# Layer two of a streaming-encoder trunk: pooling and convolution inputs with stationary weights, and eight gate pieces split by transfers

## Chip, cores and metric

One core of a Trainium2 chip runs the kernel. The metric is the device time of one execution in microseconds. The engines are PE (matrix multiplication), DVE (vector), ACT (scalar activation), POOL and SP; POOL and SP work here mainly as the two queues from which transfers are issued.

## What is computed

The reference is a trunk of two equal layers over 256 tokens of width 1024, in float32. What matters here is the first half of a layer:

```python
h = rmsnorm(x, g_pre_mix[l])
(c_q, c_kv, k_r, p_in, s_u, s_v, cv_b, cv_c, cv_x, gate_logits) = split_cols(h @ w_in[l])
y_a = mla_branch(c_q, c_kv, k_r, ...) @ w_br_a[l]
y_b = pool_branch(p_in, pool_w[l], pool_scale[l]) @ w_br_b[l]
y_c = sgu_branch(s_u, s_v, ...) @ w_br_c[l]
y_d = conv_branch(cv_b, cv_c, cv_x, conv_w[l]) @ w_br_d[l]
gates = sigmoid(gate_logits)                    # 4 branches x 1024 channels
merged = gates[:, :, 0] * y_a + gates[:, :, 1] * y_b + gates[:, :, 2] * y_c + gates[:, :, 3] * y_d
x = x + rmsnorm(merged @ w_out[l], g_post_mix[l])
```

The pooling and convolution branches work along time, so they want channels on the partitions and tokens along a row. After this half comes a feed-forward network with a gate (SwiGLU) of the same input width.

## The kernel before

Each float32 number is held as a rounded high part and a low remainder, both of a type that PE multiplies fast; a product is three matmuls, high by high, low by high, high by low (`mac`, L316 to L320). The 256 tokens are two halves `h` of 128.

All weights lie in device memory as 268 pieces of 128 x 1024 numbers in the order of their use (`piece_plan`, L79; `PLAN`). A piece passes three steps. `stage` (L247) issues a transfer from SP's queue into one of four staging tiles `st`. `convert` (L263) has ACT round it into the high tile (L268). `settle` (L283) has DVE subtract the high part from the staged piece into the low tile (L288). High and low tiles share a ring of 24 tiles `u`. `pump` (L290) converts the next piece when two of the 24 are free and keeps the transfers up to four pieces ahead; `W` (L300) hands a piece to the multiplication and frees its tiles after its last use, counted by `uses` (L112).

Work on PE is written out in order. Small generators (attention, pooling, gating, normalisation) are advanced one step at a time between the main groups by `tick` (L338), which also calls `settle` and, with fewer than six unused pieces at hand, `pump`. So the place of every instruction on every engine is fixed by the order in which the program issues it, and each engine takes its own in that order.

The start of layer two: the normalised input lies transposed in four tiles `hh0`, `hl0`, `hh1`, `hl1` (`hT_tiles`, L355), channels on partitions. Groups A (attention inputs) and S (gating unit) come first, then P (`p_in` and `cv_b`, 512 columns) and C (`cv_c` and `cv_x`, 512 columns), both by `group2` (L473) at L964 and L966: the input is the stationary operand, the weights move, and the result has tokens on partitions. ACT scales each result by the token's `rstd` when it leaves PSUM (`evict_p` L930, `evict_c` L934, where DVE also multiplies two convolution inputs). `g_misc` (L779) then turns these results with twelve PE transposes (L789, L793) and three ACT copies per half (L790, L795, L796), so that channels lie on partitions, and goes on with convolution, pooling and gating unit. Meanwhile `g_att` (L769) starts the attention: `g_proj` (L641) takes sums of squares, rotates the key part, finds the reciprocal root (`g_rsqrt`, L400, one start and three steps), scales (L658, L659), and yields `PA` ticks before it transposes.

After C follow the gates of the branches in the order d (convolution), b, c, a: for each branch two column halves of four pieces, `("gd", n, i)` first (L1027). The order of the four pieces over the two halves of tokens is (0,0) (0,1) (1,0) (1,1) (0,2) (0,3) (1,2) (1,3) (`pairs`, L458).

The feed-forward network has, for later blocks of 128 columns, another form of product (`block` L1092, `total` L1106, `g_rrow` L1082): weights stationary, input moving with high and low parts side by side, 512 columns wide, and then 256 columns for the weights' low part. The result has channels on partitions. `total` adds its two halves and multiplies by a row `rrow` that holds `rstd` per token.

Of the kernel before, what the change touches and what calls it, by code (L numbers as in the profile page):

```python
# [41 lines left out]
PA, PB = 2, 4  # L42
# [91 lines left out]
def host_piece(inp, key):  # L134
    l, g = key[0], key[1]
    cols = dict(GROUPS)
    if g in cols:
        return kxn(inp["w_in"][l], 2 * key[2], 2, cols[g])
    if g == "uq":
        return kxn(inp["w_uq"][l], key[2], 1, [c for hd in range(H) for c in q_cols(hd)])  # L140
    if g == "ukv":
        return kxn(inp["w_ukv"][l], 0, 1, [(P * hd, P * hd + 64) for hd in range(H)] +
                   [(P * hd + 64, P * hd + P) for hd in range(H)])
    if g[0] == "g":
        c = 1952 + 1024 * GATE_OF[g[1]] + 512 * key[2]
# [12 lines left out]
    raise KeyError(key)  # L158
# [38 lines left out]
def trunk(ctx: ExitStack, tc, x, xT, wall, small, const, qtab, gpost, out):  # L197
# [92 lines left out]
    def pump(n=1):  # L290

        while n and state["free"] - state["reserve"] >= 2 and state["cv"] < len(PLAN):
            settle(NST - 1)
            stage_to(min(len(PLAN), state["cv"] + NST - len(lows)))
            convert(state["cv"])
            state["cv"] += 1
            state["free"] -= 2
            n -= 1
# [55 lines left out]

    def hT_tiles(h):  # L355
        return T([P, NK, P], f"hh{h}", 1, F32R), T([P, NK, P], f"hl{h}", 1, F32R)
# [253 lines left out]
    class Part:  # L610


        def __init__(self, tiles, s, h):
            self.tiles, self.s, self.h = tiles, s, h

        def __getitem__(self, at):
            k = at[1]
            return self.tiles[k // 2][:, k % 2, self.s, self.h * P:(self.h + 1) * P]

    for l in range(NL):  # L620
# [20 lines left out]
        def g_proj():  # L641
# [24 lines left out]
            yield PA  # L666
# [112 lines left out]
        def g_misc():  # L779
            L = PAD + SEQ  # L780
            zT = tok()[:, :].rearrange("p (c t) -> p c t", c=2)
            cT_ = tok()[:, :].rearrange("p (c t) -> p c t", c=2)
            pT_ = tok()[:, :].rearrange("p (c t) -> p c t", c=2)
            nc.gpsimd.memset(pT_[:, :, 0:PAD], 0.0)
            nc.gpsimd.memset(zT[:, :, 0:PAD], 0.0)
            for h in range(2):
                o = PAD + h * P
                t = tp()
                transposes(t, [z_sb[h][:, 256 + i * P:256 + (i + 1) * P] for i in range(2)])  # L789
                nc.scalar.copy(zT[:, :, o:o + P], t[:, :256].rearrange("p (c t) -> p c t", c=2))  # L790
                yield 1
                t = tp()
                transposes(t, [p_sb[h][:, i * P:(i + 1) * P] for i in range(4)])  # L793
                t4 = t.rearrange("p (c t) -> p c t", c=4)
                nc.scalar.copy(pT_[:, :, o:o + P], t4[:, 0:2, :])  # L795
                nc.scalar.copy(cT_[:, :, o:o + P], t4[:, 2:4, :])  # L796
                yield 1
# [119 lines left out]
        else:  # L917
            o = {}
            for h, i in lead_order(8):
                if h == 1 and i == 0:  # L920
                    finish(turn)
                g, w, ev = (("A", 416, evict_a), ("S", 512, evict_s))[i // 4]
# [20 lines left out]
        pp = [mm(), mm()] if l == 0 else [acc(), acc()]  # L943
        if l == 0:
            def g_evict():
# [7 lines left out]
            for n, (h, i) in enumerate(pairs(4)):  # L953
# [26 lines left out]
        def g_merged(h, q):  # L980
            if q == 0:
# [4 lines left out]
            split_scaled(hh[:, 4 * q:4 * q + 4, :].rearrange("p k t -> p (k t)"),  # L986
                         hl[:, 4 * q:4 * q + 4, :].rearrange("p k t -> p (k t)"), t, 0.5)
# [94 lines left out]
        def g_rrow():  # L1082

            rb = tok()
            for h in range(2):
                nc.vector.tensor_copy(rb[:, h * P:(h + 1) * P], rf[h].to_broadcast([P, P]))
            yield RW
            t = tp()
            transposes(t, [rb[:, h * P:(h + 1) * P] for h in range(2)])
            nc.scalar.copy(rrow, t[:, :SEQ])  # L1090

        def block(key):  # L1092

            pc_ = W((l,) + key)
            o = mm()
            for k in range(NK):
                nc.tensor.matmul(o, pc_[0][:, k * P:(k + 1) * P], hx[k // 2][:, k % 2].rearrange("p s t -> p (s t)"),  # L1097
                                 start=(k == 0), stop=False)
                if k == 5:
                    tick()  # L1100
            for k in range(NK):
                nc.tensor.matmul(o[:, :SEQ], pc_[1][:, k * P:(k + 1) * P], hx[k // 2][:, k % 2, 0, :], start=False,  # L1102
                                 stop=(k == NK - 1))
            return o

        def total(dst, o):  # L1106
            nc.scalar.copy(dst, o[:, SEQ:2 * SEQ])  # L1107
            nc.vector.tensor_tensor(dst, o[:, 0:SEQ], dst, op=ALU.add)  # L1108
            nc.vector.tensor_tensor(dst, dst, rrow, op=ALU.mult)

        def gate_up(b):
            v, sg_ = tok(), tok()
            gv, uv = v[:, 0:SEQ], v[:, SEQ:2 * SEQ]
            o = block(("wg", b))
            if b == B0:
                finish(rr)
            total(gv, o)
# [3 lines left out]
            total(uv, block(("wu", b)))  # L1121
# [19 lines left out]

        gact = [None, None]
        pb, a = {}, {}
        for h, u in lead_order(8):
            if u == 0:
                finish(gturn[h])
                if h == 1:
                    rr = spawn(g_rrow(), 1)
# [81 lines left out]
```

## Time and profile before

| what | value |
|---|---|
| median of 3 runs | 802.87 us (802.28 to 803.49) |
| the profiled execution's own time | 802.21 us |
| its span in the trace | 800.4 us |
| PE busy | 790.8 us (99%) |
| DVE busy | 598.3 us (75%) |
| ACT busy | 452.6 us (57%) |
| POOL busy | 3.9 us (0%) |

The time is that of the whole execution; the span runs from the first to the last instruction of the trace, and the 1.8 us between them lie around it. A busy share is a mean over stages. Matmuls are pipelined, so the recorded duration of one overlaps the next, and the distance between starts tells what one costs. A row of a timeline gives start, duration, engine, line, operation, result and operands, count, and in brackets the idle time before it with what ended it.

### The profile page before, as it was taken

How to read it: one execution, taken by the hardware profiler on the slowest of the kernel's cores; microseconds unless marked ns; L12 is line 12 of the kernel's file. 1: busy time of each engine (PE TensorE's matmuls, PEld its weight loads, DVE VectorE, ACT ScalarE, POOL GpSimd, SP SyncE). 2: the span in 40 equal slices, each digit the busy share in tenths (PEclk: the TensorE clock that was granted, in tenths of full speed). 3: DMA queues.
4: the chain of work that ended last, by engine and by line, in shares of the span. 5: the costliest groups of instructions: out<-in, count | busy, mean ns of one | idle time of the engine just before them, and what ended most of it. 6: DMA issues, size and time to landing. Idle time of an engine off the chain costs nothing.

```text
span 800.4 us, 10903 instructions
## 1 busy us (share of the span) xinstructions
PE 790.8 (99%) x3982; PEld 666.3 (83%) x3982; DVE 598.3 (75%) x1094; ACT 452.6 (57%) x776; POOL 3.9 (0%) x16
## 2 busy tenths in 40 slices
PE   8999999999999999999999999999999999999996
PEld 8888887888888888888888888878888888888885
DVE  6687976758887777778895688764679787777773
ACT  7767655444665555455665675644367555455541
POOL 0000000000000000000000000000000000000000
PEclk9999999999999999999999999999999999999999
DMA  9866444465664565555655545455555555555631
GB/s 317 304 215 212 160 158 158 160 208 164 201 214 136 185 205 185 186 192 176 223 170 197 205 161 182 131 172 197 175 193 184 181 185 186 187 185 185 206 106 52
DMA packets 42245, 148.11 MB, mean 185 GB/s; under 512 B 4688, under 2 KB 5840, under 8 KB 42192
## 3 DMA queue, kind: packets, MB, share of 16 engines
q1 hardware_dynamic: 41328, 145.12, 54.4%
q0 software_dynamic: 576, 2.10, 0.8%
q8 instruction: 31, 0.51, 0.3%
q10 hardware_dynamic: 288, 0.21, 0.1%
q14 instruction: 22, 0.18, 0.1%
HBM read 146.36 MB, written 1.05 MB: 184 GB/s over the span
## 4 chain that ended last, share of the span: by engine, by line
PE 98%; DVE 1%; DMA 0%; ACT 0%; issue 0%; DVEq 0%; SPq 0%; ACTq 0%
PE acc L318 20%; PE acc L320 20%; PE acc L319 20%; PE mm L1097 17%; PE mm L1102 9%; PE tp L440 3%; PE mm L318 2%; PE mm L320 2%; PE mm L319 2%; PE mm L715 1%; PE acc L743 1%; PE acc L909 1%; DMA st<-wall 0%; PE mm L836 0%; PE mm L862 0%; DVE mrg L500 0%
## 5 line engine op out<-in xcount | busy, mean ns | idle before, releaser
L288 DVE TENSOR_TENSOR u<-st,u 128x1024 fp32r<-128x1024 f32 (+1 forms) x268 | 318.6, 1214 | 50.6 <-ACT u L268 50.0
L268 ACT ACTIVATE u<-st 128x1024 fp32r<-128x1024 f32 (+1 forms) x268 | 273.5, 1047 | 17.0 <-DMA st<-wall 16.8
L318 PE MATMUL acc<-u,hh 128*128 128x512 f32 (+1 forms) x424 | 169.1, 399 | 0.0
L320 PE MATMUL acc<-u,hh 128*128 128x512 f32 (+1 forms) x424 | 164.5, 388 | 0.0
L319 PE MATMUL acc<-u,hl 128*128 128x512 f32 (+1 forms) x424 | 164.2, 387 | 0.0
L1097 PE MATMUL mm<-u,u 128*128 128x512 f32 x576 | 144.4, 392 | 0.0
L1097 PEld LDWEIGHTS mm<-u,u 128*128 128x128 f32 x576 | 105.3, 188 | 20.8
L318 PE MATMUL acc<-u,s2k 128*128 128x512 f32 x256 | 101.2, 395 | 0.0
L320 PE MATMUL acc<-u,s2k 128*128 128x512 f32 x256 | 100.6, 393 | 0.0
L319 PE MATMUL acc<-u,s2k 128*128 128x512 f32 x256 | 100.3, 392 | 0.0
L320 PEld LDWEIGHTS acc<-u,hh 128*128 128x128 f32 x424 | 79.6, 188 | 16.2
L318 PEld LDWEIGHTS acc<-u,hh 128*128 128x128 f32 x424 | 79.7, 188 | 14.5 <-issue 0.3
L319 PEld LDWEIGHTS acc<-u,hl 128*128 128x128 f32 x424 | 79.8, 188 | 14.2
L1102 PEld LDWEIGHTS mm<-u,u 128*128 128x128 f32 x576 | 78.6, 190 | 5.6
L1102 PE MATMUL mm<-u,u 128*128 128x256 f32 x576 | 80.3, 282 | 0.0
L1025 ACT ACTIVATE gate<-acc,rhalf 128x512 f32<-128x512 f32 x32 | 22.0, 689 | 65.9 <-PE acc L320 65.7
L320 PEld LDWEIGHTS acc<-u,s2k 128*128 128x128 f32 x256 | 48.1, 188 | 10.1
L318 PEld LDWEIGHTS acc<-u,s2k 128*128 128x128 f32 x256 | 48.2, 188 | 9.3 <-issue 0.3
L319 PEld LDWEIGHTS acc<-u,s2k 128*128 128x128 f32 x256 | 48.1, 188 | 9.1
L1108 DVE TENSOR_TENSOR tok<-mm,tok 128x256 f32<-128x256 f32 x72 | 30.3, 420 | 27.7 <-ACT tok L1107 27.5
L1107 ACT COPY tok<-mm 128x256 f32<-128x256 f32 x72 | 26.6, 370 | 42.6 <-PE mm L1102 39.6
L443 ACT ACTIVATE s2k<-tok 128x256 fp32r<-128x256 f32 (+1 forms) x38 | 16.3, 429 | 53.8 <-DVE tok L1122 53.8
(172 smaller groups left out, 750.1 us busy)
## 6 DMA issues: line engine op xcount, KB each, us to landing
st<-wall SPq DMA_DIRECT2D x261, 512.0 KB, 3.8
st<-wall SPq DMA_DIRECT2D x7, 416.0 KB, 4.0
gpost<-gpost POOLq DMA_DIRECT2D x4, 512.0 KB, 4.7
x<-x SPq DMA_DIRECT2D x2, 512.0 KB, 6.0
small<-small SPq DMA_DIRECT2D x2, 512.0 KB, 4.2
u<-xT SPq DMA_DIRECT2D x3, 256.0 KB, 6.2
st<-wall SPq DMA_DIRECT2D x2, 256.0 KB, 4.3
out<-x SPq DMA_DIRECT2D x2, 256.0 KB, 2.0
```

The source lines that it names most:

```text
L268: nc.scalar.activation(hi[:, :w], st[:, :w], AF.Copy)
L288: nc.vector.tensor_tensor(lo[:, :w], st[:, :w], hi.bitcast(F32)[:, :w], op=ALU.subtract)
L318: nc.tensor.matmul(out_, a[0][aw], w[0][ws], start=start, stop=False)
L319: nc.tensor.matmul(out_, a[1][aw], w[0][ws], start=False, stop=False)
L320: nc.tensor.matmul(out_, a[0][aw], w[1][ws], start=False, stop=stop)
L440: nc.tensor.transpose(dst[:, i * P:(i + 1) * P], s, ident)
L443: nc.scalar.activation(hi, src, AF.Copy)
L1025: nc.scalar.activation(gt[h], pgt[h], AF.Tanh, scale=rhalf[h])
L1097: nc.tensor.matmul(o, pc_[0][:, k * P:(k + 1) * P], hx[k // 2][:, k % 2].rearrange("p s t -> p (s t)"), start=(k == 0), stop=False)
L1102: nc.tensor.matmul(o[:, :SEQ], pc_[1][:, k * P:(k + 1) * P], hx[k // 2][:, k % 2, 0, :], start=False, stop=(k == NK - 1))
L1107: nc.scalar.copy(dst, o[:, SEQ:2 * SEQ])
L1108: nc.vector.tensor_tensor(dst, o[:, 0:SEQ], dst, op=ALU.add)
```

## The change

In layer two only:

1. The P and C groups become eight blocks of 128 columns in the form of the feed-forward network. A piece `(1, "P", i)` or `(1, "C", i)` now holds one block with all of its 1024 rows, and is used once. The input of both halves lies in one tile `hx` of the same total size.
2. `evict_pc` brings each block out with `total`: an ACT copy, a DVE addition, a DVE multiplication by a row `row1` of `rstd` (which `g_rrow` makes beforehand with two transposes), and one further DVE multiplication for the two blocks that are multiplied with another. The results lie at once where `g_misc` put them before, so the twelve transposes and six copies fall away.
3. The eight pieces `("gd", n, i)` of layer two skip the staging tiles: POOL issues a transfer from memory into the high tile (it converts the type on the way), ACT writes the negated high part into the low tile, and POOL issues a second transfer of the same piece that adds to the low tile. DVE has no part in it.
4. `PA` in layer two is three ticks instead of two.

```diff
-PA, PB = 2, 4
+PA, PB = (2, 3), 4
...
-    if key[1] in ("wg", "wu"):
+    if key[1] in ("wg", "wu") or key[0] == 1 and key[1] in ("P", "C"):
         return 1
...
+    if l == 1 and g in ("P", "C"):
+        c = [a + P * i for a, b in cols[g] for i in range((b - a) // P)][key[2]]
+        return kxn(inp["w_in"][l], 0, NK, [(c, c + P)])
...
+        if by_dma(i):
+            state["free"] -= 1
+            staged[i] = U([P, PIECE], F32R)
+            nc.gpsimd.dma_start(staged[i], wall[i, :, :])
+            return
...
+    def by_dma(i):
+
+        key = PLAN[i][0]
+        return key[0] == 1 and key[1] == "gd"
+
     def convert(i):
         key, w = PLAN[i]
+        if by_dma(i):
+            hi, lo = staged.pop(i), U([P, PIECE], F32R)
+            nc.scalar.activation(lo, hi.bitcast(F32), AF.Copy, scale=-1.0)
+            nc.gpsimd.dma_start(lo, wall[i, :, :], accum_op=ALU.add)
+            known(i, hi, lo)
+            return
...
+    def block(key, o, both, high, mid=None):
+
+        pc_ = W(key)
+        for k in range(NK):
+            nc.tensor.matmul(o, pc_[0][:, k * P:(k + 1) * P], both(k), start=(k == 0), stop=False)
...
+        for k in range(NK):
+            nc.tensor.matmul(o[:, :SEQ], pc_[1][:, k * P:(k + 1) * P], high(k), start=False, stop=(k == NK - 1))
+        return o
+
+    def total(dst, o, tmp, rrow):
+
+        nc.scalar.copy(tmp, o[:, SEQ:2 * SEQ])
+        nc.vector.tensor_tensor(tmp, o[:, 0:SEQ], tmp, op=ALU.add)
+        nc.vector.tensor_tensor(dst, tmp, rrow, op=ALU.mult)
...
-            yield PA
+            yield PA[l]
...
-            group2(l, ("P",), hT, pp, 512, evict_p)
-        pc = [acc(), acc()]
-        group2(l, ("C",), hT, pc, 512, evict_c)
...
+                if g == "C" and i >= 2:
+                    total(v[:, 0:SEQ], o, v[:, 0:SEQ], row)
+                    nc.vector.tensor_tensor(dst, dst, v[:, 0:SEQ], op=ALU.mult)
+                else:
+                    total(dst, o, v[:, 0:SEQ], row)
+
+            for i in range(4):
+                o = block((l, "P", i), tp() if i == 2 else mm(), both, high)
+                finish(rr)
+                evict_pc("P", i, o)
+                tick()
+            for i in range(4):
+                evict_pc("C", i, block((l, "C", i), acc(), both, high))
+                tick()
```

On PE, the last block of C and the first two gate pieces of branch d now stand as follows (`L673` is the low part of a block, `L476` a transpose of the attention; `L337`, `L338`, `L339` are the three matmuls of `mac`; the low parts of the first and second gate piece are `u_878` and `u_884`):

```order
L673 MATMUL acc_4353<-hx_3822,u_874_4264 128x256 x8
L476 MATMUL tp_4384<-ident_69,u_805_3949 128x128 x3
L337 MATMUL acc_4405<-u_849_4177,hx_3822 128x512
L338 MATMUL acc_4405<-u_849_4177,hx_3822 128x512
L339 MATMUL acc_4405<-u_878_4296,hx_3822 128x512
L337 MATMUL acc_4405<-u_849_4177,hx_3822 128x512
L338 MATMUL acc_4405<-u_849_4177,hx_3822 128x512
L339 MATMUL acc_4405<-u_878_4296,hx_3822 128x512
L476 MATMUL tp_4413<-ident_69,u_805_3949 128x128 x3
L337 MATMUL acc_4405<-u_854_4204,hx_3822 128x512
L338 MATMUL acc_4405<-u_854_4204,hx_3822 128x512
L339 MATMUL acc_4405<-u_884_4335,hx_3822 128x512
```

Before, the first gate piece stood behind the second half of C with one triple of transposes between two of its units; now both triples stand beside the gate pieces, and the first two low parts are read from the third matmul of their units on.

On ACT, from the copy of the second C block to the negated copy of the fourth gate piece (`L678` is the copy of `total`, `L720`/`L721` scale the attention inputs, `L280` writes a negated high part, `L483` splits a transposed attention input), the order is now:

```order
L678 COPY tok_4309<-acc_4284 128x256
L720 ACTIVATE u_805_3949<-u_805_3949,ry_4256 128x256
L721 ACTIVATE u_805_3949<-u_805_3949,ry_4256 128x128
L720 ACTIVATE u_805_3949<-u_805_3949,ry_4256 128x256
L721 ACTIVATE u_805_3949<-u_805_3949,ry_4256 128x128
L280 ACTIVATE u_884_4335<-u_854_4204 128x1024
L678 COPY tok_4348<-acc_4316 128x256
L280 ACTIVATE u_888_4362<-u_872_4261 128x1024
L678 COPY tok_4375<-acc_4353 128x256
L483 ACTIVATE s2k_4380<-tp_4384,cst_70 128x128 x2
L483 ACTIVATE s2k_4381<-tp_4384,cst_70 128x128
```

Before, the rounding of a gate piece stood behind the same four scalings (`L658`, `L659`), and DVE's subtraction finished the piece. Now the negated copies stand there, and each is followed by a transfer. The negated copy of the fourth gate piece (`u_905`) stands behind six splits (three of them shown).

On DVE the scalings' factor `ry` is made by steps of three small instructions (`L453` to `L455`), and the additions and multiplications of the C blocks (`L679`, `L680`) now stand between these:

```order
L679 TENSOR_TENSOR tok_4276<-acc_4248,tok_4276 128x256
L680 TENSOR_TENSOR tok_4111<-tok_4276,rrow_3906 128x256
L453 TENSOR_TENSOR ra_4257<-ry_4256 128x4
L454 TENSOR_TENSOR ra_4257<-ra_4257,rv_4255 128x4
L455 SCALAR_TENSOR_TENSOR ry_4256<-ra_4257,ry_4256 128x4
L307 TENSOR_TENSOR u_874_4264<-st_4150,u_873_4263 128x1024
L453 TENSOR_TENSOR ra_4257<-ry_4256 128x4
L454 TENSOR_TENSOR ra_4257<-ra_4257,rv_4255 128x4
L455 SCALAR_TENSOR_TENSOR ry_4256<-ra_4257,ry_4256 128x4
L679 TENSOR_TENSOR tok_4309<-acc_4284,tok_4309 128x256
L680 TENSOR_TENSOR tok_4111<-tok_4309,rrow_3906 128x256
L453 TENSOR_TENSOR ra_4257<-ry_4256 128x4
```

Before, two subtractions of weights (`L288`) and no eviction stood between the same steps. The step that begins with the last row shown is the one for which the four scalings wait.

## Rows read from the trace of the kernel before

**Rows 1.** The page's busy times, and its chain that ended last, by engine.

```profile
PE 790.8 (99%) x3982; PEld 666.3 (83%) x3982; DVE 598.3 (75%) x1094; ACT 452.6 (57%) x776; POOL 3.9 (0%) x16
...
PE 98%; DVE 1%; DMA 0%; ACT 0%; issue 0%; DVEq 0%; SPq 0%; ACTq 0%
```

**Rows 2.** Busy us by stretch: length, PE, weight loads, DVE, ACT, POOL, clock, DMA.

```profile
420.00:440.00 20.00, 20.00 (x90) 16.51 (x89) 10.99 (x30) 10.47 (x20) 0.00 (x0) 1.00 0.58 196
440.00:460.00 20.00, 20.00 (x119) 17.49 (x118) 13.52 (x21) 13.09 (x26) 1.02 (x4) 1.00 0.60 208
```

**Rows 3.** Timeline of PE: group S, second half, and the first matmul of group P.

```profile
414.37 0.39 PE L318 MATMUL acc<-u,hh 128*128 128x512 f32 x1
...
421.17 0.39 PE L318 MATMUL acc<-u,hh 128*128 128x512 f32 x1
```

**Rows 4.** The chain in order of time: one block of the feed-forward network, and the next.

```profile
363.34 1.84 PE mm L1097 x8
365.18 0.95 PE mm L1102 x8
366.13 1.84 PE mm L1097 x8
```

**Rows 5.** Timeline of PE: two transposes among matmuls; twelve matmuls of 256 columns.

```profile
448.01 0.38 PE L440 MATMUL tp<-ident,tok 128*128 128x128 f32 x2
448.15 0.48 PE L318 MATMUL acc<-u,hh 128*128 128x512 f32 x1
448.46 0.39 PE L319 MATMUL acc<-u,hl 128*128 128x512 f32 x1
...
449.62 0.28 PE L318 MATMUL mm<-s2k,u 128*128 128x256 f32 x1
...
450.92 0.28 PE L320 MATMUL mm<-s2k,u 128*128 128x256 f32 x1
```

**Rows 6.** Timeline of all engines where a feed-forward block ends.

```profile
648.78 2.00 PE L1097 MATMUL mm<-u,u 128*128 128x512 f32 x8
648.98 0.37 ACT L1107 COPY tok<-mm 128x256 f32<-128x256 f32 x1 [0.53 <-PE mm L1102]
649.38 0.42 DVE L1108 TENSOR_TENSOR tok<-mm,tok 128x256 f32<-128x256 f32 x1
649.84 0.42 DVE L1109 TENSOR_TENSOR tok<-tok,rrow 128x256 f32<-128x256 f32 x1
```

**Rows 7.** Timeline of DVE during group C.

```profile
432.34 0.29 DVE L632 TENSOR_TENSOR tok<-u,cst 128x32 f32<-128x32 f32 x2
...
433.74 0.25 DVE L650 COPY kr<-kr 128x96 f32<-128x96 f32 x1
...
435.26 0.15 DVE L417 TENSOR_TENSOR ra<-ry 128x4 f32<-128x4 f32 x1
...
435.75 1.22 DVE L288 TENSOR_TENSOR u<-st,u 128x1024 fp32r<-128x1024 f32 x1
...
439.27 2.46 DVE L665 COPY u<-tp 64x1024 f32<-64x1024 f32 x2 [0.19 <-PE tp L440]
```

**Rows 8.** Timeline of ACT: scalings, the rounding of a gate piece, splits.

```profile
439.12 0.51 ACT L658 ACTIVATE u<-u,ry 128x256 f32<-128x256 f32 x1 [2.47 <-DVE ry L419]
...
440.52 1.05 ACT L268 ACTIVATE u<-st 128x1024 fp32r<-128x1024 f32 x1
...
447.22 0.37 ACT L447 ACTIVATE s2k<-tp,cst 128x128 fp32r<-128x128 f32 x1 [1.58 <-DVE s2k L448]
448.01 0.37 ACT L447 ACTIVATE s2k<-tp,cst 128x128 fp32r<-128x128 f32 x1 [0.42 <-DVE s2k L448]
```

**Rows 9.** Transfers: SP's queue (packets, MB, share of 16 engines), and issues (count, size, us to landing).

```profile
q1 hardware_dynamic: 41328, 145.12, 54.4%
...
st<-wall SPq DMA_DIRECT2D x261, 512.0 KB, 3.8
...
gpost<-gpost POOLq DMA_DIRECT2D x4, 512.0 KB, 4.7
```

**Rows 10.** The tile gpost: its four transfers from POOL's queue.

```profile
DMA to landing us min/median/max: 3.8/4.7/4.9
```

More of the change, by code (lines that the diff above doesn't have):

```diff
@@ L353, in finish, with __init__, __getitem__ @@
             advance(e)
+    class Part:
+        def __init__(self, tiles, s, h):
+            self.tiles, self.s, self.h = tiles, s, h
+        def __getitem__(self, at):
+            k = at[1]
+            c = np.s_[self.s, self.h * P:(self.h + 1) * P]
+            if len(self.tiles) == 1:
+                return self.tiles[0][:, k, c[0], c[1]]
+            return self.tiles[k // 2][:, k % 2, c[0], c[1]]
+    hx_now = [None]
     def hT_tiles(h):
-        return T([P, NK, P], f"hh{h}", 1, F32R), T([P, NK, P], f"hl{h}", 1, F32R)
+        if h == 0:
+            hx_now[0] = T([P, NK, 2, SEQ], "hx", 1, F32R)
+        return tuple(Part([hx_now[0]], s, h) for s in range(2))
     ident = T([P, P], "ident", 1, pool=cp)
@@ L608, in trunk, with rows_in, rows_out, g_rrow @@
     turn = None
[L610 to L618, printed above, removed]
+    def rows_in(rs):
+        rb = tok()
+        for h in range(2):
+            nc.vector.tensor_copy(rb[:, h * P:(h + 1) * P], rs[h].to_broadcast([P, P]))
+        return rb
+    def rows_out(rrow, rb):
+        t = tp()
+        transposes(t, [rb[:, h * P:(h + 1) * P] for h in range(2)])
+        nc.scalar.copy(rrow, t[:, :SEQ])
+    def g_rrow(rrow, rs):
+        rb = rows_in(rs)
+        yield RW
+        rows_out(rrow, rb)
+    def block(key, o, both, high, mid=None):
+        pc_ = W(key)
+        for k in range(NK):
+            nc.tensor.matmul(o, pc_[0][:, k * P:(k + 1) * P], both(k), start=(k == 0), stop=False)
+            if k == 5:
+                if mid is not None:
+                    mid()
+                tick()
[6 more added lines that the diff above has]
+        nc.vector.tensor_tensor(dst, tmp, rrow, op=ALU.mult)
     for l in range(NL):
@@ L780, in g_misc @@
             L = PAD + SEQ
[L781 to L797, printed above, removed]
+            if l == 0:
+                zT = tok()[:, :].rearrange("p (c t) -> p c t", c=2)
+                cT_ = tok()[:, :].rearrange("p (c t) -> p c t", c=2)
+                pT_ = tok()[:, :].rearrange("p (c t) -> p c t", c=2)
+                nc.gpsimd.memset(pT_[:, :, 0:PAD], 0.0)
+                nc.gpsimd.memset(zT[:, :, 0:PAD], 0.0)
+                for h in range(2):
+                    o = PAD + h * P
+                    t = tp()
+                    transposes(t, [z_sb[h][:, 256 + i * P:256 + (i + 1) * P] for i in range(2)])
+                    nc.scalar.copy(zT[:, :, o:o + P], t[:, :256].rearrange("p (c t) -> p c t", c=2))
+                    yield 1
+                    t = tp()
+                    transposes(t, [p_sb[h][:, i * P:(i + 1) * P] for i in range(4)])
+                    t4 = t.rearrange("p (c t) -> p c t", c=4)
+                    nc.scalar.copy(pT_[:, :, o:o + P], t4[:, 0:2, :])
+                    nc.scalar.copy(cT_[:, :, o:o + P], t4[:, 2:4, :])
+                    yield 1
+            else:
+                zT, cT_, pT_ = zcp
             dh = T([P, 2, SEQ], "s2k", 10, F32R)
@@ L962, in trunk, with both, high, evict_pc @@
                 tick()
-        else:
-            group2(l, ("P",), hT, pp, 512, evict_p)
-        pc = [acc(), acc()]
-        group2(l, ("C",), hT, pc, 512, evict_c)
+            pc = [acc(), acc()]
+            group2(l, ("C",), hT, pc, 512, evict_c)
+        else:
+            zcp = [tok()[:, :].rearrange("p (c t) -> p c t", c=2) for _ in range(3)]
+            for i in (0, 2):
+                nc.gpsimd.memset(zcp[i][:, :, 0:PAD], 0.0)
+            row = row1
+            htile = hx_now[0]
+            def both(k):
+                return htile[:, k].rearrange("p s t -> p (s t)")
+            def high(k):
+                return htile[:, k, 0, :]
+            def evict_pc(g, i, o):
+                dst = zcp[(2 if i < 2 else 1) if g == "P" else 0][:, i % 2, PAD:PAD + SEQ]
+                v = tok()
+                if g == "C" and i >= 2:
+                    total(v[:, 0:SEQ], o, v[:, 0:SEQ], row)
+                    nc.vector.tensor_tensor(dst, dst, v[:, 0:SEQ], op=ALU.mult)
+                else:
+                    total(dst, o, v[:, 0:SEQ], row)
[6 more added lines that the diff above has]
+                evict_pc("C", i, block((l, "C", i), acc(), both, high))
+                tick()
         sm = small_load(l)
@@ L1080, in trunk @@
         rrow = T([P, SEQ], "rrow", 1)
[L1082 to L1109, printed above, removed]
         def gate_up(b):
```

21 lines of the change are left out of this document (13 added, 8 removed).

## Prediction

> **What bounds the kernel now.** I read the page first, then busy time by stretch, then timelines of PE, ACT and DVE around the place of the change. PE is busy for 790.8 of 800.4 us, and the chain that ended last is PE's to 98% [rows 1]. In the two stretches around groups P and C, PE is busy for 20.00 of 20.00 us at full clock, while DVE has 10.99 and 13.52, ACT 10.47 and 13.09, and DMA 0.58 and 0.60 [rows 2]. So no wait is left there to remove. The time changes only with what PE has to do, or with a wait that the change adds. What DVE saves is worth nothing by itself.
>
> **PE's own work.** Groups P and C were 96 matmuls of 512 columns. Thirty such starts lie between 414.37 and 421.17 us, so one costs 0.2267 us [rows 3], and 96 cost 21.76. They become eight blocks of eight matmuls of 512 and eight of 256 columns; such a block takes 366.13 - 363.34 = 2.79 us [rows 4], eight 22.32. That is **+0.56 us**: the columns are the same in number (96 x 512 = 64 x 512 + 64 x 256), so turning the operands saves nothing on PE. Twelve transposes go and two come (for the row of `rstd`). Two transposes put off the matmul behind the next one by 448.46 - 448.01 - 0.227 = 0.22 us [rows 5], 0.11 each; ten fewer are **-1.1 us**. PE's work thus changes by -0.5 us.
>
> **The eviction of blocks and the eight DVE subtractions.** DVE gains eight subtractions of 1.22 us [rows 7] and loses about as much to sixteen additions and multiplications of 0.46 and two products more, less what `evict_c` did. ACT copies 256 columns eight times and loses six turned copies. All of it lies beside PE; if that cover went, it would show as a wait of PE. The transposes' row, the memory of `hx` and the piece layout cost nothing more: the same bytes come on the same queue, and pieces of P and C are read well after they are made.
>
> **The wait that is added.** Before, a gate piece was finished by a subtraction of 1.22 us behind ACT's rounding. Now a transfer L stands in its place, issued by POOL only when ACT has written the negated part. POOL's queue is not what holds it; ACT is, and ACT waits for DVE. I follow the order given above with durations from rows. Group P begins at 421.17 us [rows 3]; two transposes first, so block four ends at 421.17 + 0.22 + 4 x 2.79 = 432.55.
>
> - ACT's copy starts 0.20 us after a block's end, DVE's addition 0.40 behind that, its multiplication 0.46 later [rows 6]: DVE is through with block four at 432.55 + 0.20 + 0.40 + 0.92 = 434.07.
> - DVE then rotates the keys, 433.99 - 432.34 = 1.65; subtracts a weight piece, 1.22; starts the root, 0.49 as a step takes (435.26 to 435.75) [rows 7]; adds and multiplies C's first block, 0.92; one step, 0.49; subtracts, 1.22; one step; C's second block, 0.92; the last step. Sum 7.89: 441.96. (The second block ends at 438.1, so DVE and not PE is late.)
> - ACT scales four times, 1.40, and writes the second gate piece's negated part, 1.05 [rows 8]: the transfer leaves at 444.4.
> - PE wants that piece's low part at 421.17 + 0.22 + 22.32 for the blocks, + 0.22 and 0.66 for eight transposes, + 8 x 0.2267 = 446.4.
>
> So the second piece has 2.0 us for its transfer. For the fourth: ACT copies a block, writes the third piece's negated part (445.8), copies the last block (446.15). DVE, after 2.46 us of key copies [rows 7], does three instructions of 0.46 for each of two blocks, until 447.6. Then splits alternate between ACT and DVE at 0.79 us [rows 8]; with four such turns and two small scalings the fourth negated part is written from 451.0 to 452.1. PE wants it 24 matmuls of 512 columns and twelve of 256 (0.118 each [rows 5]) after the second, at 446.4 + 5.44 + 1.42 = 453.3, plus whatever PE has waited. That leaves 1.2 us. The splits follow transposes that stand ahead of PE's first wait, so that wait doesn't delay them. PE therefore waits **L - 2.0** at the second piece, and after the fourth **L - 1.2 in all**. The first piece has some seven us, the third 4.8 and the wait, those of the second column half over eight: nothing is added there.
>
> **L.** No transfer of the trace adds to its target. The nearest row is `gpost`, 512 KB from the same queue: 3.8 to 4.9, median 4.7 us [rows 9, 10]; a plain piece on SP's queue takes 3.8 [rows 9]. An adding transfer also reads its target. SP's queue moved 145.12 MB in 54.4% of 800.4 us, 333 GB/s, so one more pass over 524288 bytes is 1.6 us: 6.3 if nothing overlaps. I take **5.5**, midway between 4.7 and 6.3. The ends kept are 3.8, a plain landing, and 9.4, two `gpost` landings one after the other.
>
> The Trainium skill ("DMA: Bandwidth & Descriptors", "Anatomy of one DMA — SWDGE (gpsimd) path") fits such a transfer as 2.0 us plus bytes over 436 GB/s. By that L would be an estimated 3.2 us, the wait 2.0 and the time 804.4; the trace's four `gpost` transfers of that size took longer, at least 3.8 us.
>
> **Sum.** -0.5 + (5.5 - 1.2) = +3.8 us. The profiled execution took 802.21, so it would take 806.0; the median of the runs stands 0.66 above it, and 802.87 + 3.8 gives **806.7 us**. With L at 3.8 and 9.4 it is 805.0 and 810.6.
>
> **Rivals.** *No difference* (0.2%, that is 1.6 us, is about what a measurement of this kernel can tell from none). It needs a wait under 2.1 us, L under 3.3, or ACT further ahead than I follow it. For: my chain has some fifteen terms, each good to a few hundredths, and DVE may find its staged pieces earlier. Against: no 512 KB transfer here lands in 3.3 us. Time 802.3 to 804.4; chance 0.20.
>
> *Not slower*: the wait vanishes because DVE reaches the last step of the root early. The place is the three steps between the C blocks; the point is the second negated part written 5.5 us before 446.4, at 440.9 instead of 444.4, and the fourth 4.3 us earlier. Then only PE's -0.5 us is left, 802.3, and at most -1.1 us, 801.8, if the blocks cost what the groups did. Against: the second C block ends only at 438.1, and its eviction, a step, four scalings and the copy (0.6 + 0.92 + 0.49 + 1.40 + 1.05) already end at 442.6. This is part of the case above; that it goes below 801.3 has no row for it, chance 0.06.
>
> *Transfers as the bound*: eight pieces are read twice and eight targets once. Sixteen extra passes of 1.6 us are 25 us of all DMA engines within some 40 us in which 0.4 is free, 16 us. If the nine us of overrun all reach PE besides the 0.5 saved, the time is about 811 to 815. For: POOL's and SP's transfers share the engines. Against: pieces behind these eight are staged over ten us ahead. Chance 0.08.
>
> **How the numbers follow.** The forecast has 0.66, no difference 0.20, a clear gain 0.06, the overload 0.08. Slower by over 0.2% takes the forecast and the overload, 0.74; the same 0.20; faster 0.06. The range runs from 802.2, where the wait is hidden and PE's saving stays, to 811.0, just above L = 9.4. The forecast alone, which holds most of the chance, has 804.4 to 810.6.
>
> **What would show it.** Right: PE idle ahead of the third matmul of the second gate piece, by 2 to 7 us, released by a transfer from POOL, and a smaller gap at the fourth; eight blocks 2.79 us apart; ten transposes fewer; DVE with eight subtractions fewer and still no wait on it. Wrong: PE still without a gap after group C, or its gap ahead of other tiles (staged pieces, PSUM tiles); the adding transfers landing in under 3.3 us; the negated parts written well before 444 us of the old time; blocks slower than 2.79 us.

## The result and the profile after

The changed kernel takes **809.90 us** in the median (808.85 to 811.03), the kernel before 802.87: ratio 1.0086, 95% interval 1.0073 to 1.0100, that is 7.0 us slower. Forecast were 806.7 us and a range of 802.2 to 811.0. Direction and range hold; instead of 3.8 us it lost nearly twice as many. The profiled execution took 808.96 us, 6.75 more than that of before.

The page of the changed kernel, busy times, transfers and issues (to be read beside [rows 1, 9]):

```profile
PE 790.5 (98%) x4004; PEld 664.8 (82%) x4004; DVE 596.1 (74%) x1104; ACT 452.0 (56%) x775; POOL 15.4 (2%) x32
...
q1 hardware_dynamic: 40176, 140.92, 52.1%
q0 software_dynamic: 2880, 10.49, 5.2%
...
PE 89%; DMA 4%; issue 3%; DVE 2%; ACT 1%; POOL 1%; DVEq 0%; ACTq 0%; POOLq 0%
...
u<-wall POOLq DMA_DIRECT2D x16, 512.0 KB, 7.1
```

PE works as long as before, but the chain is PE's to 89% only, where it was 98%, and now runs through transfers, ACT and POOL too. The busy times by stretch, columns as in [rows 2], show where:

```profile
420.00:440.00 20.00, 20.00 (x114) 17.39 (x113) 13.21 (x34) 10.55 (x22) 3.04 (x5) 1.00 0.90 303
440.00:460.00 20.00, 14.18 (x77) 11.33 (x75) 11.52 (x29) 9.55 (x19) 6.86 (x10) 1.00 1.01 259
```

Where PE had 20.00 of 20.00 us it has 14.18; the clock stays at 1.00, and DMA goes from 0.60 to 1.01 (the times of all packets are added up, so the share can pass 1). In the timeline of PE three matmuls waited, each for a transfer, each the third matmul of a unit, which reads a low part. The first two rows are blocks of group P:

```profile
424.30 2.00 PE L667 MATMUL mm<-hx,u 128*128 128x512 f32 x8
...
427.09 2.00 PE L667 MATMUL tp<-hx,u 128*128 128x512 f32 x8
...
446.38 0.40 PE L338 MATMUL acc<-u,hx 128*128 128x512 f32 x1
449.77 0.50 PE L339 MATMUL acc<-u,hx 128*128 128x512 f32 x1 [2.99 <-DMA u<-wall]
...
453.75 0.39 PE L338 MATMUL acc<-u,hx 128*128 128x512 f32 x1
455.53 0.50 PE L339 MATMUL acc<-u,hx 128*128 128x512 f32 x1 [1.39 <-DMA u<-wall]
...
458.17 0.40 PE L338 MATMUL acc<-u,hx 128*128 128x512 f32 x1
460.44 0.50 PE L339 MATMUL acc<-u,hx 128*128 128x512 f32 x1 [1.88 <-DMA u<-wall]
```

From start to start these are 3.39, 1.78 and 2.27 us where 0.227 is usual: 3.16 + 1.55 + 2.05 = **6.8 us** of waits, at the second, third and fourth gate piece. Less 0.5 us of PE work that is 6.3; the last matmul starts 6.3 us later than before (799.07 against 792.74). The rest of the 6.75 lies behind it. One other wait of PE is not in the profile of before: 0.45 us at 39.5 us, for a subtraction in layer one, which the change leaves as it was.

The three transfers by themselves (line L281, one stretch each: the issue, who waited for it, and L, the time from the issue to the landing):

```profile
L281 POOL DMA_DIRECT2D u<-wall x1: 876/876/876, 444.3 to 444.3; - x1
...
  PE acc L339: 3.0, 1
...
DMA to landing us min/median/max: 5.5/5.5/5.5
...
L281 POOL DMA_DIRECT2D u<-wall x1: 1118/1118/1118, 445.5 to 445.5; - x1
...
  PE acc L339: 1.4, 1
...
DMA to landing us min/median/max: 10.0/10.0/10.0
...
L281 POOL DMA_DIRECT2D u<-wall x1: 887/887/887, 451.5 to 451.5; - x1
...
  PE acc L339: 1.9, 1
...
DMA to landing us min/median/max: 8.9/8.9/8.9
```

The second piece's transfer takes the 5.5 us that I took for L. The third's takes 10.0 and the fourth's 8.9. The queues in the stretch from 440 to 460 us (packets, MB, share of 16 engines) show what the engines had to do meanwhile:

```profile
q0 software_dynamic: 1273, 4.65, 93.9%
q1 hardware_dynamic: 144, 0.52, 6.5%
```

POOL's queue (q0) alone nearly fills the engines; SP's (q1) moves one piece.

### The profile page after: what moved, and what is told of

Read it like the earlier page. It is cut to its first block, busy times and chain, and to the rows that moved or that the text cites. A ratio compares the mean times of both kernels' runs of the same rounds, so it can differ in the third digit from the quotient of the medians.

```text
span 807.2 us, 10985 instructions
## 1 busy us (share of the span) xinstructions
PE 790.5 (98%) x4004; PEld 664.8 (82%) x4004; DVE 596.1 (74%) x1104; ACT 452.0 (56%) x775; POOL 15.4 (2%) x32
## 3 DMA queue, kind: packets, MB, share of 16 engines
q1 hardware_dynamic: 40176, 140.92, 52.1%
## 4 chain that ended last, share of the span: by engine, by line
PE 89%; DMA 4%; issue 3%; DVE 2%; ACT 1%; POOL 1%; DVEq 0%; ACTq 0%; POOLq 0%
PE acc L339 18%; PE acc L337 18%; PE acc L338 18%; PE mm L667 17%; PE mm L673 9%; PE tp L476 3%; DMA st<-wall 2%; PE mm L337 2%; PE mm L339 2%; PE mm L338 2%; PE mm L777 1%; DMA u<-wall 1%; DVE u L307 1%; PE acc L805 1%; ACT u L287 1%
## 5 line engine op out<-in xcount | busy, mean ns | idle before, releaser
L307 DVE TENSOR_TENSOR u<-st,u 128x1024 fp32r<-128x1024 f32 (+1 forms) x260 | 309.3, 1214 | 43.6 <-ACT u L287 43.3
L287 ACT ACTIVATE u<-st 128x1024 fp32r<-128x1024 f32 (+1 forms) x260 | 265.3, 1047 | 17.6 <-DMA st<-wall 17.0
L339 PE MATMUL acc<-u,hx 128*128 128x512 f32 (+1 forms) x392 | 152.6, 389 | 6.7 <-DMA u<-wall 6.3
L337 PE MATMUL acc<-u,hx 128*128 128x512 f32 (+1 forms) x392 | 156.4, 399 | 0.0
L338 PE MATMUL acc<-u,hx 128*128 128x512 f32 (+1 forms) x392 | 151.8, 387 | 0.0
L337 PE MATMUL acc<-u,s2k 128*128 128x512 f32 x256 | 100.9, 394 | 0.0
L339 PE MATMUL acc<-u,s2k 128*128 128x512 f32 x256 | 100.6, 393 | 0.0
L338 PE MATMUL acc<-u,s2k 128*128 128x512 f32 x256 | 100.4, 392 | 0.0
L339 PEld LDWEIGHTS acc<-u,hx 128*128 128x128 f32 x392 | 73.6, 188 | 23.9 <-DMA u<-wall 7.6
L337 PEld LDWEIGHTS acc<-u,hx 128*128 128x128 f32 x392 | 73.7, 188 | 13.2 <-issue 0.5
L338 PEld LDWEIGHTS acc<-u,hx 128*128 128x128 f32 x392 | 73.7, 188 | 13.0
L673 PEld LDWEIGHTS mm<-u,u 128*128 128x128 f32 x576 | 78.6, 190 | 5.6
L673 PE MATMUL mm<-u,u 128*128 128x256 f32 x576 | 80.3, 282 | 0.0
L339 PEld LDWEIGHTS acc<-u,s2k 128*128 128x128 f32 x256 | 48.1, 188 | 10.0
L679 DVE TENSOR_TENSOR tok<-mm,tok 128x256 f32<-128x256 f32 x75 | 31.5, 421 | 33.2 <-ACT tok L678 33.0
L337 PEld LDWEIGHTS acc<-u,s2k 128*128 128x128 f32 x256 | 48.2, 188 | 9.3 <-issue 0.2
L338 PEld LDWEIGHTS acc<-u,s2k 128*128 128x128 f32 x256 | 48.1, 188 | 9.2
L678 ACT COPY tok<-mm 128x256 f32<-128x256 f32 x75 | 27.7, 370 | 46.6 <-PE mm L673 43.7
```

What stands on the lines that cost most here:

```text
L307: nc.vector.tensor_tensor(lo[:, :w], st[:, :w], hi.bitcast(F32)[:, :w], op=ALU.subtract)
L337: nc.tensor.matmul(out_, a[0][aw], w[0][ws], start=start, stop=False)
L338: nc.tensor.matmul(out_, a[1][aw], w[0][ws], start=False, stop=False)
L339: nc.tensor.matmul(out_, a[0][aw], w[1][ws], start=False, stop=stop)
L678: nc.scalar.copy(tmp, o[:, SEQ:2 * SEQ])
L679: nc.vector.tensor_tensor(tmp, o[:, 0:SEQ], tmp, op=ALU.add)
```

## The experiments

Two questions were open: which part of the change brings the 7 us, and whether the third and fourth transfer are slow in themselves, late, or in a full queue. The table has the median, the ratio to the kernel before with its interval, and the waits of PE from 440 us on that I read in the profile (start to start, less the usual distance). Small gaps beside a wait, under 0.4 us each, are counted with it in e8, e9, e11 and e12.

| run | kernel | us | ratio (95%) | waits, us |
|---|---|---|---|---|
| | changed | 809.90 | 1.0086 (1.0073 to 1.0100) | 6.8 |
| e1 | layout only | 804.51 | 1.0023 (1.0012 to 1.0035) | 2.3 |
| e2 | transfers only | 808.38 | 1.0068 (1.0053 to 1.0084) | 3.8 + 0.8 |
| e3 | second transfer plain | 807.28 | 1.0054 (1.0040 to 1.0069) | 3.8 + clock |
| e5 | one copy earlier | 808.11 | 1.0068 (1.0054 to 1.0082) | 4.2 + clock |
| e10 | all copies earlier | 807.19 | 1.0059 (1.0044 to 1.0075) | 3.7 + clock |
| e6 | transfers, first half | 805.97 | 1.0040 (1.0026 to 1.0053) | 3.3 |
| e4 | transfers, second half | 803.49 | 1.0011 (1.0002 to 1.0020) | 1.6 |
| e7 | layout, key copies on ACT | 804.10 | 1.0016 (1.0008 to 1.0025) | 2.0 |
| e8 | layout, earlier conversion | 805.30 | 1.0037 (1.0024 to 1.0049) | 2.6 |
| e9 | second half, earlier | 803.60 | 1.0015 (1.0006 to 1.0024) | 1.5 |
| e11 | e9, key copies on ACT | 804.03 | 1.0019 (1.0010 to 1.0028) | 1.7 |
| e12 | e11, one piece earlier | 803.05 | 1.0010 (1.0001 to 1.0019) | 1.4 |

**The parts alone: e1 and e2.** In e1 `by_dma` is false for all pieces; e2 is the kernel before with `by_dma` and its two branches.

```diff
-        return key[0] == 1 and key[1] == "gd"
+        return False
```

> The changed kernel with the eight gate pieces back on the old path (staging tile, ACT rounding, DVE subtraction); pooling and convolution blocks stay as changed. Theory (the loss lies only in three PE waits on adding transfers): those waits, 3.16 + 1.55 + 2.05 = 6.8 us, are gone and PE's own saving of 0.5 us stays: 802.3 us, ratio to the kernel before 0.9993, PE without a gap from 440 to 465 us. Rival (the blocks themselves or their evictions cost, DVE now having blocks and subtractions in one stretch): PE waits on a subtraction or a PSUM tile there, 804 to 810 us.

> The kernel before with only the eight gate pieces by transfers; pooling and convolution groups as before. Theory: the waits come with the transfers alone. The second negated copy ends at about 441.6, its transfer leaves at 441.8 and PE wants it at 444.3, 2.5 us later, so with 5.4 us a wait of 2.9, and further waits at the third and fourth pieces as in the changed kernel, 6 to 7 us in all: 809 to 810 us. Rival (the blocks of the changed kernel make the negated copies late, so that the old groups leave time enough): at most 3 us, 803 to 806.

e1 was slower by 1.7 us, not faster by 0.5: the rival holds. Its timeline of PE:

```profile
448.49 0.50 PE L339 MATMUL acc<-u,hx 128*128 128x512 f32 x1 [0.77 <-DVE u L307]
456.49 0.50 PE L339 MATMUL acc<-u,hx 128*128 128x512 f32 x1 [0.53 <-DVE u L307]
460.99 0.38 PE L337 MATMUL mm<-s2k,u 128*128 128x256 f32 x1 [0.54 <-DVE u L748]
```

DVE is late. The busy times from 434 to 453 us, columns as in [rows 2], before and in e1:

```profile
434.00:453.00 19.00, 19.00 (x99) 15.92 (x98) 14.62 (x31) 12.19 (x26) 1.02 (x4) 1.00 0.58 205
```

```profile
434.00:453.00 19.00, 18.23 (x99) 15.21 (x98) 17.20 (x47) 9.64 (x25) 0.00 (x0) 1.00 0.45 166
```

DVE has 17.20 of 19 us instead of 14.62, in order: the evictions of the blocks stand there beside the subtractions of the gate pieces. In the changed kernel the transfers take these subtractions away, so no wait on DVE shows. e2, the transfers alone, loses 5.6 us, 0.6 below its range: two waits on transfers (2.01 and 1.77 us), and 0.8 us on a product of DVE at 484; where the last us of the loss lies was not found. The times of the two parts add up to about the whole, 1.7 + 5.6 = 7.3 us against 7.0, but the waits behind them are not the same: the changed kernel has none of e1's waits on DVE, and waits 6.8 us on transfers where e2 waits 3.8. In e2 the second piece's transfer left 4.9 us before PE wanted it (441.86 and 446.77), in the changed kernel, where the evictions stand ahead of it on DVE, only 2.4.

**Slow, late or in a queue: e3, e5, e10, e6.** e3 drops the addition; e5 converts one piece earlier; e10 converts all of them earlier; e6 leaves the second half to the old path.

```diff
-            nc.gpsimd.dma_start(lo, wall[i, :, :], accum_op=ALU.add)
+            nc.gpsimd.dma_start(lo, wall[i, :, :])
```

> The changed kernel, but the second transfer writes the piece plainly over the negated copy instead of adding to it; left out is the subtraction of the high part (the low tile holds the whole weight). Same count of transfers, same bytes from memory, same waits and order. In the changed kernel an adding packet of 4 KB takes 328 ns in the middle, a plain or converting one 174. Theory (adding packets take twice as long and fill all DMA engines from 446 us on, which stretches the third and fourth landings to 9 to 10 us): the eight transfers take 8 x 128 x (328 - 174) / 16 = 9.9 us less of all engines; landings of 4 to 5 us, the fourth piece's transfer (leaves at 451.5, wanted at 453.7 without waits) lands at about 456: waits of 2 to 3 us in all, 804.5 to 805.5 us. Rival (a transfer from this queue takes its time whatever it does, what counts is when it leaves): landings of 5.4 to 10 us as now, 808.5 to 810.5.

```diff
-            for _ in g_rsqrt(res, m, 4):
-                yield 1
+            for n, _ in enumerate(g_rsqrt(res, m, 4)):
+                yield pump() or 1 if (l, n) == (1, 3) else 1
```

> The changed kernel with one swap on ACT: the second gate piece's negated copy stands ahead of the four scalings instead of behind them. It then runs at about 438.8 and its transfer leaves at 440.0 instead of 444.25; all else is in the same order. Rival A (only the lateness of a transfer counts, each takes 5.4 us): the second lands at 445.5, before it is wanted at 446.6, the third at 450.9 without a wait, the fourth (leaves at 451.5) at 456.9 against 453.7: one wait of 3.2 us, 805.6 us. Theory (DMA engines are full from 440 us on, the fourth landing is set by the sum of bytes in the queue): the first wait goes, but the later ones take its place, the fourth piece still lands at 458.5 to 460.5: 5 to 6.8 us in all, 807.5 to 809.5 us. Rival B: the second transfer lands no earlier, since the engines serve the first piece's transfer and other pieces up to then: nothing changes, 809.9.

```diff
-                evict_pc("C", i, block((l, "C", i), acc(), both, high))
+                o = block((l, "C", i), acc(), both, high)
+                if i >= 1:
+                    pump()
+                settle()
+                evict_pc("C", i, o)
                 tick()
```

> The changed kernel (all eight gate pieces by transfers) converted earlier in the same way: the second adding transfer leaves at about 440, the third at 444, the fourth at 445.6 instead of 444.25, 445.5 and 451.5. Theory (POOL's queue is served in order and the engines are full from 440 on): the second lands at about 450 to 451 as in the run with one earlier copy, the third at 454 to 455, the fourth at 457 to 458 against a wanted 453.7: waits of 3.5 to 4.5 us, and PE's clock may fall behind a wait of 4 us: 805.5 to 808 us. Rival (lateness is all, a transfer takes 5.4 us from its issue): the fourth lands at 451, no wait is left, 802.3 to 803 us.

```diff
-        return key[0] == 1 and key[1] == "gd"
+        return key[0] == 1 and key[1] == "gd" and key[2] == 0
```

> The changed kernel with transfers only for the four pieces of the first column half; those of the second half go the old way (staging, rounding, subtraction). On POOL's queue the converting transfers of the second half no longer stand between the adding ones. Theory (the queue serves transfers in the order of issue, an adding one alone takes 5.4 to 5.5 us and each transfer ahead of it costs 1.4 to 2.7 us more): the second piece is as late as before (leaves about 444.2, lands 449.7, wait 3.2 us), the third lands at 452 to 453 without a wait of its own, the fourth (leaves 451.5) at 457 to 457.5, a wait of 0.1 to 0.6 more: 3.3 to 3.8 us of waits, and up to 0.9 us for a DVE that again subtracts four pieces: 805.5 to 807 us. Rival (each adding transfer is slow by itself, 9 to 10 us from the third on, whatever stands beside it): 809 to 810 us. Rival B (a wait of 3 us or more also lowers the clock of PE and that is most of the loss): 807 to 809 with matmuls 0.43 us apart behind the wait.

*e3* came out 1.8 us above its range. The waits at the third and fourth piece went, and POOL's queue took 4.0% of the engines' time instead of 5.2%, 9.8 us less of all sixteen, so the addition does cost that. But the second piece still waited for 3.8 us: its plain transfer landed only 6.2 us after its issue, later than the adding one in the same place (5.5), and no run shows why. Behind the wait the matmuls ran 0.43 us apart. By stretch in e3, columns as in [rows 2]:

```profile
445.00:449.00 4.00, 0.52 (x3) 0.09 (x1) 2.24 (x9) 1.75 (x6) 1.08 (x3) 0.90 0.91 308
449.00:455.00 6.00, 5.80 (x14) 4.55 (x15) 2.89 (x6) 3.61 (x5) 2.11 (x4) 0.50 1.01 326
```

From 449.20 to 454.91 us thirteen distances take 5.71 instead of 2.95, so the clock costs 2.8 us there. The wait and the clock together are 6.6 us, of which the median shows less: this one execution was 1.1 us ahead of that of before already at 84 us.

*e5* lies within its forecast (807.5 to 809.5), by another path than written. The transfer left at 440.3 and landed no earlier than in the changed kernel (449.7):

```profile
L281 POOL DMA_DIRECT2D u<-wall x1: 873/873/873, 440.3 to 440.3; - x1
...
DMA to landing us min/median/max: 10.6/10.6/10.6
```

This is rival B for that piece: PE waited there, once, for 4.2 us, and the clock took 1.7 more; no later piece made it wait for more than 0.1 us. Rival A, by which only the time of issue counts, would have given 805.6 and falls. *e10* says the same of all of them: the second and the fourth transfer were issued 5.5 and 5.8 us earlier than in the changed kernel (438.75 and 445.72) and took 11.4 and 13.3 us, so that the fourth landed at 459.0 instead of 460.4, and the time is 807.2 us; lateness alone would have given 802.3 to 803.

*e6* takes the second half's transfers from between the adding ones. It came out at 805.97, in the range of the theory. In its profile the third and the fourth transfer land in 6.5 and 5.4 us:

```profile
L281 POOL DMA_DIRECT2D u<-wall x1: 868/868/868, 445.4 to 445.4; - x1
...
DMA to landing us min/median/max: 6.5/6.5/6.5
...
L281 POOL DMA_DIRECT2D u<-wall x1: 870/870/870, 451.4 to 451.4; - x1
...
DMA to landing us min/median/max: 5.4/5.4/5.4
```

So an adding transfer isn't slow by itself from the third on. In the changed kernel landings follow the order of issue: 449.7 (444.25 + 5.5), 451.7 (a converting one, 444.8 + 6.9), 455.5, 456.8 (`gpost`), 458.0 (converting), 460.4. The third piece's transfer landed 3.8 us behind the one ahead of it and the fourth's 2.4: most of their 10.0 and 8.9 us had passed before the one ahead was done.

What stands ahead is not all, though. The first piece's adding transfer has nothing ahead of it in POOL's queue; its L was 6.1 us in the changed kernel, 6.6 in e6, 7.1 in e5 and 8.0 in e10. The converting transfer behind it (line L258) has that one ahead of it each time, and yet took longer in e5, where two more were issued within 2.6 us behind it; in the changed kernel, shown first, the next came 6 us later:

```profile
L258 POOL DMA_DIRECT2D u<-wall x1: 896/896/896, 438.1 to 438.1; - x1
...
DMA to landing us min/median/max: 7.0/7.0/7.0
```

```profile
L258 POOL DMA_DIRECT2D u<-wall x1: 893/893/893, 438.3 to 438.3; - x1
...
DMA to landing us min/median/max: 9.8/9.8/9.8
```

And a staged piece that SP's queue issued beside them (at 439.8, 440.0 and 438.7 us) took 6.4 us in the changed kernel, 9.1 in e5 and 7.6 in e10, where the median before was 3.8. So the order in POOL's queue does not account for all of it. That the sixteen engines, which both queues share, had more to do at once is the likely reason, but it was not tested alone: e6 takes away transfers ahead and lowers that load as well (0.80 of the engines from 440 to 460 us, not 1.01), and no run tells what each of the two makes of the 10.0 and 8.9 us.

**The second half alone, and the layout's own wait: e4, e7, e8, e9, e11, e12.** e4 has `key[2] == 1` where e6 has 0.

> The changed kernel with transfers only for the four pieces of the second column half; the first half goes the old way. Theory: the second half's transfers are wanted over 8 us after they leave, so no wait of PE ends with a transfer; what is left is the lateness of DVE that the layout-only kernel showed at the second and fourth piece (0.94 + 0.70 us, 0.70 behind): 803.5 to 804.8 us. Rival (any transfers from POOL's queue in this stretch delay the staged pieces or each other so that PE waits): 806 to 809 us.

No wait of PE ends with a transfer there; the two waits on DVE (0.94 + 0.70 us) stay, and 803.49 fits. The others try to take the wait from DVE. e7 is e1 with the key copies on ACT; e8 and e9 are e1 and e4 with the edit of e10; e11 is e9 with the edit of e7; e12 is e11 with `i == 1` for `i >= 1`.

```diff
+            transposes(t, [krs[h].rearrange("p n d -> p (n d)") for h in range(2)])
+            kT[:] = [keep([P, 4, SEQ]) for _ in range(2)]
+            for e in range(2):
+                rows = slice(64 - 64 * e, P - 64 * e)
+                (nc.vector.tensor_copy if l == 0 else nc.scalar.copy)(
+                    kT[e][rows], t[rows, 0:SEQ].unsqueeze(1).to_broadcast([64, 4, SEQ]))
             for h in range(2):
                 nc.scalar.activation(a_sb[h][:, 0:256], a_sb[h][:, 0:256], AF.Identity, scale=r4[:, 2 * h:2 * h + 1])
...
-            transposes(t, [krs[h].rearrange("p n d -> p (n d)") for h in range(2)])
...
```

> The layout-only kernel (no transfers) with the two copies of the turned keys (64 x 1024, 2.46 us of DVE together) moved from DVE to ACT in layer two, ahead of the four scalings, where ACT sat idle for 2.67 us waiting for the root. Theory (the layout costs time because DVE is late with the subtractions of the second and fourth gate pieces): DVE reaches them 0.7 to 2.4 us earlier, the three waits of 0.94, 0.70 and 0.70 us go or fall below 0.3 each, and PE's own -0.5 us shows: 802.2 to 803.0 us, ratio to the kernel before 0.9993 to 1.0002. Rival (the layout costs elsewhere, in PE's blocks or at the start of the run): 804.5 as the layout-only kernel, ratio 1.002.

> The layout-only kernel (no transfers) with weights converted earlier: ahead of the eviction of the second, third and fourth block of C a further piece is rounded and all staged subtractions are made, so that on ACT the second gate piece is rounded ahead of the four scalings and the fourth ahead of the splits. No instruction more or less. Theory (the layout costs time only because ACT and DVE come to the second and fourth gate piece too late): the waits at these two pieces (0.94 + 0.70 us) go, the one behind them (0.70, on a product with the table) goes or stays, and PE's -0.5 us shows: 802.2 to 803.0 us, ratio to before 0.9993 to 1.0002. Rival (the waits only move to other pieces, or the cost is elsewhere): 804 to 804.5 us, ratio 1.0015 to 1.0023.

> The kernel with transfers for the second column half alone, converted earlier in the same way as the layout-only one in this call. Theory: the two waits on DVE (1.64 us) go, no wait ends with a transfer, PE has 0.5 us less to do than before the change: 802.2 to 802.8 us, ratio 0.999 to 1.000, the lowest of all versions. Rival: the earlier transfers of the second half fall into the stretch of other transfers and PE waits on staged pieces: 803.5 or more.

> The kernel with transfers for the second column half and earlier conversion, with the two key copies (2.46 us) moved from DVE to ACT ahead of the four scalings, where ACT sat idle for 5.1 us. Theory (in this stretch the layout overfills DVE, so work must leave DVE, not only change places): DVE reaches the splits about 1.3 us earlier, the wait of 0.7 us and the 0.4 behind it at the projections go, 0.3 us at the transposes (root late) may stay: waits of 0 to 0.4 us against 0.5 us less work on PE: 802.2 to 802.9 us, ratio to before 0.9995 to 1.0005. Rival (DVE is not what limits, the waits move once more): 803.6 us, ratio 1.0015.

> As the other kernel of this call, but only the second gate piece is converted earlier; third and fourth at their usual places. Theory: the wait at the second piece goes, DVE has 2.46 us less, so the splits begin 0.7 to 1.3 us earlier; the fourth piece's rounding behind the splits leaves a wait of 0 to 0.5 us: 802.3 to 803.0 us, ratio 0.9995 to 1.0007. Rival: 803.6 us, ratio 1.0015.

e7, e8, e9 and e11 came out 0.8 to 2.3 us above their ranges, e12 at the edge of its own, with 0.7 us at the fourth piece where at most 0.5 was expected: the waits moved instead of going. In e7 DVE stood idle for 2.13 us, since the copy of the third block on ACT now came behind the key copies and the scalings; the three waits stayed at 0.7 us each. In e8 the root came later, ACT stood idle for 5.07 us before the scalings, and PE waited elsewhere:

```profile
445.97 0.62 PE L476 MATMUL tp<-ident,u 128*128 128x128 f32 x3 [0.23 <-ACT u L720]
454.51 0.39 PE L337 MATMUL mm<-s2k,u 128*128 128x256 f32 x1 [0.51 <-ACT s2k L483]
461.97 0.39 PE L337 MATMUL mm<-s2k,u 128*128 128x256 f32 x1 [0.93 <-DVE u L748]
```

That DVE is busier in e1 and its products late is shown; that DVE's load alone is the reason is not, for in that stretch it is 14.86 us in e12 and 14.09 in e7, where before had 14.62, and still they wait 1.4 and 2.0 us. What stays open is whether some order of ACT and DVE hides the layout's evictions. None of the thirteen beats the kernel before; e12 and e4 come nearest, 0.1% above it.

## Why the prediction was right, and what was mis-sized

- **PE's own work, -0.5 us:** right. Blocks stand 427.09 - 424.30 = 2.79 us apart, the group of transposes from `tok` counts 90 instead of 100, and waits less 0.5 account for the start of the last matmul.
- **Evictions and subtractions at nothing:** right for the changed kernel, where PE waits for nothing of DVE in layer two. But the cover is not free time of DVE, as I had it: it is the eight subtractions that the transfers take away. With them back (e1) the same evictions cost 1.7 us.
- **The chain to the second piece:** right. I had DVE through with block four at 434.07 (its next work starts at 434.08), the transfer leaving at 444.4 (444.25), PE asking at 446.4 (446.38 + 0.23 = 446.6). L - 2.0 = 3.5 was forecast, 3.16 came.
- **L:** 5.5 was right for the second piece (5.5 here, 5.1 in e6), but it is no fixed time: with nothing ahead of them in their queue adding transfers took 5.1 (e6) to 8.0 us (e10). That 5.5, midway between two rows, met the second piece so closely is in part luck. A plain one with nothing ahead took 3.5 (e3, issued at 462.5). The Trainium skill ("DMA: Bandwidth & Descriptors", "Anatomy of one DMA — SWDGE (gpsimd) path") gives an estimated 3.2 for the size; the plain one is near it, the adding one is not, and the measurement decides.
- **The step that failed** is "after the fourth L - 1.2 in all" with the same L for every piece, and with it "the third 4.8 and the wait, [...] nothing is added there". The fourth transfer left earlier than I followed it (451.5 us, not 452.1) and was wanted at 458.17 + 0.23 - 3.16 - 1.55 = 453.7, a lead of 2.2 instead of 1.2. But its L was 8.9: 8.9 - 2.2 = 6.7 us in all, which is what came. The third's L was 10.0 against a lead of 8.5, the second piece's wait included. I looked for what holds a transfer back before its issue, found that "POOL's queue is not what holds it", and did not count the transfers that are still ahead of it in the queue once it is issued: for the fourth piece an adding one, `gpost` and a converting one, the last of which landed at 458.0, 6.5 us after the fourth's issue. With those of the second half gone, and the engines less full for it (e6), L is 5.1 to 6.5 for these three pieces and the time 805.97, within 0.8 us of the forecast.
- **That the range held** is owed to its upper end: L at 9.4, two landings one after the other, which the sum itself did not count. The 7.0 us measured answer to an L of 8.7 in that sum.
- **Transfers as the bound** (0.08) had the mechanism that made the difference, but not its price. The engines were full (1.01), and POOL's twenty transfers took 5.2% of 807.2 us, 42 us of all engines. Only what delayed three low parts reached PE, not the whole overrun: 6.8 us of waits, where the rival needed 9.
- **No difference** needed L under 3.3 us and **not slower** an early root. The root's last step came 0.5 us before my 441.96, far from enough; and e10 shows that even transfers issued 5.5 us earlier would not have saved it.

## What to carry to other kernels

A transfer's time is not its own alone: for each one that somebody waits for, list what is issued ahead of it on the same queue and still under way, and add those; and where the engines are full, reckon with more: above, the same converting transfer took 9.8 us instead of 7.0 when two more were issued soon behind it. Moving work from a loaded engine to transfers pays only if the transfers' engines have room in that very stretch (0.60 before, 1.01 after). Two passes over the weights with an addition need much more of it than one load: over the whole run POOL's queue went from 0.8% of the engines' time to 5.2%, SP's only from 54.4% to 52.1%. Where two edits come together, ask of each what it costs alone: here the layout cost 1.7 us, the transfers 5.6, and both together 7.0, though PE waited for other things than in either.

## What the runs showed of the chip

With nothing ahead of it in its queue an adding transfer of 512 KB landed in 5.1 us at best (e6) and 8.0 at worst (e10), a plain one from the same queue in 3.5 at best (e3), and the eight additions took 9.8 us of all sixteen engines (5.2% of 807.2 us against 4.0% of 805.5). Transfers of POOL's queue landed in the order of issue in all fourteen traces. The Trainium skill ("DMA: Bandwidth & Descriptors", "SWDGE vs HWDGE vs iDMA") says that only one such queue is allocated, which agrees.

I had not expected the clock to take part. In e3, e5 and e10 the granted clock was 0.50, 0.57 and 0.53 in stretches of 6, 4 and 3.6 us behind a wait, the level of 1.2 GHz for most of them. PE had been idle before for 3.67 us in e3, for 3.99 in e5, and for 0.54 and 2.46 in e10. In the changed kernel's profile it was idle for 2.99 us and the clock stayed at 1.00. The rows of e5:

```profile
450.95 0.50 PE L339 MATMUL acc<-u,hx 128*128 128x512 f32 x1 [3.99 <-DMA u<-wall]
...
451.60 0.63 PE L338 MATMUL acc<-u,hx 128*128 128x512 f32 x1
452.02 0.63 PE L339 MATMUL acc<-u,hx 128*128 128x512 f32 x1
...
454.58 0.51 PE L339 MATMUL acc<-u,hx 128*128 128x512 f32 x1
454.93 0.40 PE L337 MATMUL acc<-u,hx 128*128 128x512 f32 x1
```

That is 0.42 us from start to start instead of 0.227. So behind a wait of a few microseconds more can be lost than the wait itself: 1.7 us here and 2.8 in e3. The changed kernel's other executions, of which there is no trace, may hold such falls too: the mean clock of its five was 0.994 to 0.998, and 0.998 in the profiled one and in that of the median.
